# Two layers of a mixed network with a mixture of experts: the filter spectra start ahead of the routing, and eight tiles for the first expert's weights go

## The chip, the cores and the metric

The kernel runs on one core of one Trainium2 chip. The metric is the device time of one execution in microseconds (us); lower is better. The engines are named as in the profile: PE (TensorE matmul), PEld (TensorE weight load), DVE (VectorE), ACT (ScalarE), POOL (GpSimd), SP (SyncE, which only issues transfers here). Each engine works through its own queue strictly in the order in which the program was laid out.

## The reference, cut to what matters

The network has two blocks of two layers each on 256 tokens of width 1024. The first block ends in a mixture of experts: a router picks two of eight experts for each token, and each expert is a gated feed-forward network of hidden width 3584.

```python
def moe_swiglu(h, router, wg, wu, wd):
    logits = (h @ router).astype(jnp.float32)
    top_v, top_i = lax.top_k(logits, TOP_K)
    gates = jax.nn.softmax(top_v, axis=-1)
    combine = jnp.sum(jax.nn.one_hot(top_i, N_EXPERTS, dtype=jnp.float32) * gates[..., None], axis=-2)
    for e in range(N_EXPERTS):
        y = y + combine[..., e:e + 1] * swiglu(h, wg[e], wu[e], wd[e]).astype(jnp.float32)
```

The second block needs two things that depend on no token of the first: the spectra of its long filters (a small network on 256 positions, a window, a norm, a Fourier transform), and keys and values of a memory of 256 rows for its cross attention.

```python
def hyena_filter_spectra(z, window, w1, b1, w2, b2, w3, b3, freq):
    h = jnp.sin(c(freq[0]) * (z @ c(w1) + c(b1)))
    h = jnp.sin(c(freq[1]) * (h @ c(w2) + c(b2)))
    h = (h @ c(w3) + c(b3)).reshape(L, HY_ORDER, 2, HY_WIDTH) * window[:, None, None, :]
    fwd, bwd = h[:, :, 0], h[:, :, 1]
    f = jnp.concatenate([fwd, jnp.zeros((1, HY_ORDER, HY_WIDTH), F32), bwd[1:][::-1]], axis=0)
    f = f / (jnp.sum(jnp.abs(f), axis=0, keepdims=True) + EPS)
    return jnp.fft.rfft(f, axis=0)
```

## The kernel before, in words

All stages run one after the other: a front (attention, feed-forward, a recurrent layer), the mixture of experts (`st_moe`), and two layers of the second block.

**Weights.** Three pools of tiles of 512 KB serve the whole kernel: `wt` (7), `wh` (7) and `wl` (6), 20 tiles. In the dense layers a weight is loaded into `wt` and split into a high part in `wh` and a low part in `wl`. In the mixture of experts the weights are used in float32 as they come, so that `moe_fetch` loads them into the three pools in turn. One expert has 84 such tiles, and SP issues their loads in the order of use; a load waits until the tile's former user is done. For the first fetches there are eight more tiles, `early0` to `early7`, in a pool that is opened ahead of the expert loop and closed after the first call of `moe_hidden`.

**The routing** (lines 755 to 835) transposes the tokens, multiplies by the router, takes the two best, counts the tokens of each expert (`pp` L779 to L781, `pc` L800) and ranks the experts. Then `moe_select` builds a selection matrix (`sel` L949), and `moe_gather` (L962) collects the tokens of a pair of experts by eight groups of matmuls into `hT`. The experts run in the order of `ranks`; in slots 64, 64, 96, 64, 96, 64, 96, 64 tokens wide (experts 0 to 7 below). Each has four steps s: 16 tiles of gate and up weights in `moe_hidden` (8 in the last step half as wide, so three steps of 24 and one of 12 tiles with `moe_down`, 84 in all).

**The side work.** Spectra and memory keys and values are a generator, `moe_side`; `fill()` advances it by one step. Between groups of matmuls the expert loop calls `fill()` four times a step for experts of 64 slots and three times for those of 96 (none in the very first step): 12, 16, 12, 16, 12, 16, 12, 16, in all 112 calls. The spectra have 35 steps for each of the two layers, the memory 18 for each, in all 106. Inside the expert loop PE's order is pinned to the order of the program (`in_order`). What the steps of the spectra do up to the second product of the transform, with the tags of their buffers (one buffer a tag), is:

```python
w1 = s1.tile([33, 64], F32, name="hw1", tag="hw1")
w2 = s1.tile([64, 64], F32, name="hw2", tag="hw1")
zT = s1.tile([33, T], F32, name="zT", tag="hh1")
    arg = s1.tile([64, T], F32, name="arg", tag="inv")
        w3 = s1.tile([65, 512], F32, name="w3", tag="inv")
            nc.tensor.matmul(ps, h[:65, c * P:(c + 1) * P], w3[:65], start=True, stop=True)
            nc.vector.tensor_tensor(t, ps, win[:, c], op=ALU.mult)
        S = s1.tile([P, 512], F32, name="S", tag="S")
        nc.vector.tensor_tensor(S, ps, inv, op=ALU.mult)
        nc.gpsimd.tensor_tensor(S, S, skip, op=ALU.add)
        nc.gpsimd.dma_start(self.spec[i][o][:, fc], S)
```

So `w2` takes the buffer of `w1`, the two `w3` follow each other in the buffer that `arg` had, and the second `S` takes the buffer of the first, whose transfer to DRAM must have landed. All loads of the spectra are issued by POOL.

**PSUM.** `st_moe` has the banks `mm` (3), `tp` (1), `y` (2), `yc` (1) and `gs` (1). A step of the side work that asks for a bank while it rides in `fill()` gets the one that `self.ride` names, `gs` or `yc`. The routing and the gathers use `gs` as well.

Of the kernel before, what the change touches and what calls it, by code (L numbers as in the profile page):

```python
# [8 lines left out]
F32 = mybir.dt.float32  # L9
# [7 lines left out]
P = 128  # L17
# [48 lines left out]
class KB:  # L66
# [657 lines left out]
    def st_moe(self):  # L724
        nc, tc, I = self.nc, self.tc, self.I
        E, F = 8, 3584
        with tc.tile_pool(name="moc", bufs=1) as mc, tc.tile_pool(name="mot", bufs=2) as mt, self.banks(y=2, yc=1, gs=1):
            self.side = self.moe_side()
            xn = [mc.tile([P, TC, D], FR, name=f"xn{i}") for i in range(2)]
            io8 = mc.tile([P, E], F32, name="io8")  # L730
            nc.sync.dma_start(io8, I["c_iota"][:, :E])
# [103 lines left out]
            nc.vector.tensor_copy(cnti, cnt[:, E:])  # L835

            self.mo = mc, mt, xn, ios, dup
            self.homes = cycle([(self.wp, "wt"), (self.whp, "wh"), (self.wlp, "wl")])

            ranks = (0, 4, 1, 5, 2, 6, 3, 7)  # L840
# [3 lines left out]
            def weights(i):  # L844
                q = ranks[i]
                if q == 0:
                    return [I[f"moe_{n}"][0] for n in ("gate", "up", "down")]
                if ids[i] is None:
                    ids[i] = nc.values_load(idi[0:1, q - 1:q], engines=(mybir.EngineType.SP,), min_val=1, max_val=E - 1)
                return [I[f"moe_{n}"][bass.ds(ids[i], 1)].rearrange("o t p n -> (o t) p n") for n in ("gate", "up", "down")]  # L850
# [2 lines left out]
            pair = self.moe_select(ranks[:2], posr)  # L853
            for k in range(KC):
                self.moe_gather(pair, k)

            early = tc.tile_pool(name="early", bufs=1)
            ep = early.__enter__()
            self.early = iter([ep.tile([P, 1024], F32, name=f"early{i}") for i in range(8)])

            prev, scatter, nxt = None, [], None
            with self.in_order():
                for i, s in order:
                    j = i % 2
                    short = slots[i] == 64
                    jobs = {}
                    job = lambda g, f: jobs.setdefault(g, []).append(f)
                    if prev:
                        job(0, lambda o=prev: self.moe_turn(o))
                        job(1, lambda o=prev: self.moe_turn_c(o))  # L870
                    if s == 0 and prev:
                        back = self.moe_back(prev, posr, Gr, ranks[i - 1])
                        next(back)
                        job(2, lambda: next(back))
                        job(3, lambda: next(back))
                    if s == 1:
                        for g, f in enumerate(scatter):
                            job(g, f)
                    if j == 1 and i + 1 < E and s >= 2:
                        if s == 2:  # L880
                            nxt = self.moe_select(ranks[i + 1:i + 3], posr)
                        for g in range(4):
                            job(g, lambda k=4 * (s - 2) + g: self.moe_gather(nxt, k))
                    self.ride = "yc" if short and s else "gs"
                    if i or s:
                        for g in (1, 3, 4, 5) if short else (1, 3, 5):
                            job(g, self.fill)
                    one = self.moe_hidden(pair, j, weights(i), s, jobs, slots[i])
                    if not prev:
                        early.__exit__(None, None, None)  # L890
                    else:
                        scatter = self.moe_down(prev, jobs)
                    prev = one
                    if s == len(self.MOE_S) - 1 and j == 1 and i + 1 < E:
                        pair = nxt
                self.ride = "gs"
                back = self.moe_back(prev, posr, Gr, ranks[-1])
                next(back)
                self.moe_turn(prev)
                next(back)  # L900
                self.moe_turn_c(prev)
                next(back)
                self.fill(99)
                for f in self.moe_down(prev, {}):
                    f()
# [76 lines left out]

    def moe_fetch(self, src, a):

        t = next(self.early, None)
        if t is None:
            pool, tag = next(self.homes)
            t = pool.tile([P, 1024], F32, name=tag, tag=tag)
        self.nc.sync.dma_start(t, src)
        t = t.rearrange("p (a b) -> p a b", a=a)  # L990
        return [t[:, i] for i in range(a)]
# [962 lines left out]
```

## Time and profile before

| what | value |
|---|---|
| median of 3 runs | 2669.59 us (2655.94 to 2670.45) |
| the profiled execution | 2667.7 us, its span 2665.9 us, 1.8 us around it |
| PE busy | 2554.8 us, 96% of the span |
| mean granted TensorE clock | 0.979 of full speed |
| HBM read | 620.97 MB |

Matmuls are pipelined and their ends are modelled, so that a high busy share of PE does not say that PE is the bound. Where the DMA share (mean busy share of the 16 DMA engines) stands at 1.00, the stream of weights is the bound whatever PE's share is.

### The profile page before, as it was taken

To read this page: it belongs to the slowest core of one execution; us is meant where nothing else is said; L and a number is where in the kernel's file an instruction comes from. 1 tells how busy PE (TensorE), PEld (TensorE's weight loads), DVE (VectorE), ACT (ScalarE), POOL (GpSimd) and SP (SyncE) were. 2 spreads that over 40 slices of the span, in tenths; PEclk is the share of its full clock that TensorE was granted. 3 is DMA by queue.
4 is the path that set the end of the run, shared out by engine and by line. 5 is a ranking of instruction groups with operands and counts; after the bars stand their busy time and mean duration, and the time that the engine had idled before them with its cause. 6 is when DMAs were issued, how large, how long until landed. Compare 5 with 4: busy or idle time off the path is not lost. (4 is left out here: it accounts for less than half of the span.)

```text
span 2665.9 us, 34015 instructions
## 1 busy us (share of the span) xinstructions
PE 2554.8 (96%) x12437; PEld 1625.0 (61%) x12437; DVE 1146.4 (43%) x1838; ACT 1032.8 (39%) x1751; POOL 228.4 (9%) x354
## 2 busy tenths in 40 slices
PE   8999999899999999899999879999999999999999
PEld 6788877433433423354344357777777767777777
DVE  6655574222112211212122065757644657656544
ACT  6544464101101110222122065546654655546543
POOL 1000000111200211000000030100100111001000
PEclk9999997899999999899999989999999999999999
DMA  5555552799999999798988955335455544444553
GB/s 160 175 190 184 178 163 94 284 405 415 416 389 386 417 384 337 299 348 305 359 304 308 375 171 158 122 122 197 147 171 186 162 141 136 141 145 161 175 181 103
DMA packets 237218, 632.73 MB, mean 237 GB/s; under 512 B 31070, under 2 KB 38228, under 8 KB 236532
## 3 DMA queue, kind: packets, MB, share of 16 engines
q1 hardware_dynamic: 232628, 618.62, 65.0%
q0 software_dynamic: 4128, 11.67, 1.1%
q8 instruction: 100, 1.64, 0.2%
q14 instruction: 74, 0.61, 0.1%
q10 hardware_dynamic: 288, 0.19, 0.0%
HBM read 620.97 MB, written 9.44 MB: 236 GB/s over the span
## 5 line engine op out<-in xcount | busy, mean ns | idle before, releaser
L165 DVE TENSOR_TENSOR wl<-wt,wh 128x1024 fp32r<-128x1024 f32 (+2 forms) x477 | 578.6, 1219 | 323.5 <-PE mm L157 151.3
L164 ACT ACTIVATE wh<-wt 128x1024 fp32r<-128x1024 f32 (+2 forms) x477 | 495.3, 1053 | 256.2 <-PE y L158 138.0
L156 PE MATMUL mm<-wh,hTh 128*128 128x512 f32 (+2 forms) x1104 | 438.6, 398 | 4.3 <-ACT hTh L167 3.0
L158 PE MATMUL mm<-wh,hTl 128*128 128x512 f32 (+2 forms) x1104 | 434.6, 395 | 2.6 <-DVE hTl L168 2.5
L157 PE MATMUL mm<-wl,hTh 128*128 128x512 f32 (+2 forms) x1104 | 433.5, 393 | 0.4 <-DVE wl L165 0.4
L156 PEld LDWEIGHTS mm<-wh,hTh 128*128 128x128 f32 x1104 | 209.8, 190 | 54.0 <-ACT hTh L167 7.3
L158 PEld LDWEIGHTS mm<-wh,hTl 128*128 128x128 f32 x1104 | 209.3, 190 | 47.9 <-DVE hTl L168 5.2
L157 PEld LDWEIGHTS mm<-wl,hTh 128*128 128x128 f32 x1104 | 209.8, 190 | 42.9 <-issue 2.4
L1006 PE MATMUL mm<-wl,hT 128*64 128x512 f32 (+1 forms) x724 | 175.1, 556 | 3.4 <-DMA wl<-in_moe_up 2.5
L1006 PE MATMUL mm<-wt,hT 128*64 128x512 f32 (+1 forms) x692 | 162.6, 541 | 4.2 <-DMA wt<-in_moe_up 4.2
L1096 PE MATMUL y<-wh,aT 128*64 128x512 f32 x348 | 164.7, 606 | 1.4 <-DMA wh<-in_moe_down 1.3
L1006 PE MATMUL mm<-wh,hT 128*64 128x512 f32 (+1 forms) x600 | 147.4, 562 | 8.1 <-DMA wh<-in_moe_up 5.1
L156 PE MATMUL y<-wh,ah 128*128 128x512 f32 x368 | 147.3, 403 | 1.7 <-ACT ah L164 1.7
L158 PE MATMUL y<-wh,al 128*128 128x512 f32 x368 | 144.8, 400 | 0.0
L157 PE MATMUL y<-wl,ah 128*128 128x512 f32 x368 | 143.7, 396 | 0.0
L1096 PE MATMUL y<-wt,aT 128*64 128x512 f32 x292 | 138.7, 605 | 0.2 <-DMA wt<-in_moe_down 0.2
L1096 PE MATMUL y<-wl,aT 128*64 128x512 f32 x256 | 121.5, 601 | 2.4 <-DMA wl<-in_moe_down 2.3
L1006 PEld LDWEIGHTS mm<-wl,hT 128*64 128x64 f32 x724 | 48.7, 138 | 87.2 <-issue 65.1
L1014 ACT ACTIVATE sg<-mm 128x512 f32<-128x512 f32 (+1 forms) x32 | 17.4, 543 | 206.3 <-PE mm L1006 206.2
L1006 PEld LDWEIGHTS mm<-wt,hT 128*64 128x64 f32 x692 | 47.6, 138 | 76.4 <-issue 58.3
L1031 DVE COPY aT<-tp 128x512 f32<-128x512 f32 (+1 forms) x32 | 20.0, 624 | 167.9 <-PE tp L1029 167.9
L1006 PEld LDWEIGHTS mm<-wh,hT 128*64 128x64 f32 x600 | 41.7, 139 | 78.7 <-issue 61.9
(659 smaller groups left out, 3852.6 us busy)
## 6 DMA issues: line engine op xcount, KB each, us to landing
wt<-in_mlp_w SPq DMA_DIRECT2D x128, 512.0 KB, 4.4
wt<-in_w_in SPq DMA_DIRECT2D x104, 512.0 KB, 4.5
wh<-in_moe_down SPq DMA_DIRECT2D x87, 512.0 KB, 9.8
wl<-in_moe_gate SPq DMA_DIRECT2D x79, 512.0 KB, 9.5
wt<-in_moe_gate SPq DMA_DIRECT2D x78, 512.0 KB, 7.7
wl<-in_moe_up SPq DMA_DIRECT2D x78, 512.0 KB, 9.4
wt<-in_moe_down SPq DMA_DIRECT2D x73, 512.0 KB, 9.2
wt<-in_moe_up SPq DMA_DIRECT2D x71, 512.0 KB, 9.9
```

The source lines that it names most:

```text
L156: nc.tensor.matmul(ps, a[0], b[0], start=start, stop=False)
L157: nc.tensor.matmul(ps, a[0], b[1], start=False, stop=False)
L158: nc.tensor.matmul(ps, a[1], b[0], start=False, stop=stop)
L164: nc.scalar.activation(hi, src, AF.Copy)
L165: nc.vector.tensor_tensor(lo, src, hi.bitcast(F32), op=ALU.subtract)
L1006: nc.tensor.matmul(bank[i][64 * z:64 * z + 64, :W], hT[:, k, :64], gu[i][k - k0][:, z * W:(z + 1) * W], start=k == 0, stop=k == KC - 1)
L1014: nc.scalar.activation(a[:, :W], bank[0][:, :W], AF.Silu)
L1031: nc.vector.tensor_copy(o["aT"][:, :nj], pt[:, :nj * P].rearrange("p (j t) -> p j t", j=nj))
L1096: nc.tensor.matmul(y[n][64 * z:64 * z + 64], aT[:, j, 64 * z:64 * z + 64], w[j - j0][z][:, n * 512:(n + 1) * 512], start=first and j == 0, ...
```

## The change

The side work gets its first step at the head of `st_moe`, ahead of the routing in the program, and fourteen more behind the routing, ahead of the first gather. `self.ride` is `gs` for those. The pool `early` and its eight tiles are gone, so that the first fetches go to the 20 tiles of the three pools. The number of `fill()` calls in the expert loop stays.

```diff
@@ st_moe
             self.side = self.moe_side()
+            self.fill()
             xn = [mc.tile([P, TC, D], FR, name=f"xn{i}") for i in range(2)]
...
             self.mo = mc, mt, xn, ios, dup
+            self.ride = "gs"
+            self.fill(14)
             self.homes = cycle([(self.wp, "wt"), (self.whp, "wh"), (self.wlp, "wl")])
...
             pair = self.moe_select(ranks[:2], posr)
             for k in range(KC):
                 self.moe_gather(pair, k)
-
-            early = tc.tile_pool(name="early", bufs=1)
-            ep = early.__enter__()
-            self.early = iter([ep.tile([P, 1024], F32, name=f"early{i}") for i in range(8)])
...
                     one = self.moe_hidden(pair, j, weights(i), s, jobs, slots[i])
-                    if not prev:
-                        early.__exit__(None, None, None)
-                    else:
+                    if prev:
                         scatter = self.moe_down(prev, jobs)
@@ moe_fetch
-        t = next(self.early, None)
-        if t is None:
-            pool, tag = next(self.homes)
-            t = pool.tile([P, 1024], F32, name=tag, tag=tag)
+        pool, tag = next(self.homes)
+        t = pool.tile([P, 1024], F32, name=tag, tag=tag)
```

On PE the place is between the counts of the routing (`gs<-M,tri`) and the first gather (`gs<-sel,xn`). Before, the queue read:

```order
L781 MATMUL gs<-M,tri 128x8
L800 MATMUL gs<-M,tri 128x8 x2
L962 MATMUL gs<-sel,xn_3943 128x256
L962 MATMUL gs<-sel,xn_3944 128x256
...
L1006 MATMUL mm<-early_4157,hT 64x512
```

With the change it reads as follows; L1163 are the two layers of the small network, L1184 its output for two directions and two halves of the tokens, L1222 and L1232 the norm, L156 to L158 the products of the transform:

```order
L782 MATMUL gs<-M,tri 128x8
L801 MATMUL gs<-M,tri 128x8 x2
L1163 MATMUL gs<-zT,hw_3950 64x256
L1163 MATMUL gs<-hh,hw_3952 64x256
L1184 MATMUL gs<-w_4147,hh 128x512 x2
L1184 MATMUL gs<-w_4162,hh 128x512 x2
L1222 MATMUL gs<-ones,acc 128x1 x4
L1232 MATMUL gs<-ident,inv_4195 128x128 x4
L156 MATMUL gs<-pmh,dfh 128x512
...
L158 MATMUL gs<-pmh,dfl 128x512
L959 MATMUL gs<-sel,xn_3958 128x256
```

All of the matmuls of the fifteen steps (two products of six matmuls at their end) now stand in one piece ahead of the first gather, and none between two matmuls of the routing.

On POOL the place is the same stretch of the program. Before, the norm of the tokens (`ss`, `rm`, `rs`) and the scaled tokens `xn` came first:

```order
L188 TENSOR_TENSOR ss_4009<-ss 128x1
L175 TENSOR_SCALAR rm<-ss_4009 128x1
L177 TENSOR_TENSOR rs<-rm,mhalf 128x1
L786 TENSOR_SCALAR xn_3943<-x,rs 128x1024
L380 DMA win<-in_c_win 128x2x512
L382 DMA fwd<-in_c_dft 128x1024
```

With the change the first loads stand ahead of them, and all that follows to the second `S` behind them:

```order
L380 DMA win<-in_c_win 128x2x512
L382 DMA fwd<-in_c_dft 128x1024
L1152 DMA hw_3950<-in_hy_w_2 33x64
L1156 DMA zT<-in_c_zT 33x256
...
L787 TENSOR_SCALAR xn_3958<-x,rs 128x1024
L1154 DMA hw_3952<-in_hy_w_2 64x64
...
L1179 DMA w_4147<-in_hy_w_2 64x512
...
L1242 DMA spec_88<-S 128x512
L1241 TENSOR_TENSOR S<-S,skip 128x512
```

The loads of `win`, `fwd`, `hw` and `zT` moved ahead of the norm of the tokens; the order among the steps of the spectra stayed.

## Rows read from the trace of the kernel before

**Rows 1.** Windows by stage: length, busy time of each engine, clock, DMA share, GB/s.
```profile
480.00:494.00 14.00, 6.96 (x38) 6.63 (x38) 7.03 (x46) 0.37 (x2) 2.68 (x1) 0.62 0.93 378
494.00:512.20 18.20, 17.64 (x72) 8.18 (x74) 1.76 (x11) 3.79 (x8) 0.58 (x1) 0.83 0.00 1
512.20:924.60 412.40, 399.94 (x2096) 149.93 (x2092) 80.88 (x159) 50.40 (x95) 56.45 (x70) 0.99 1.01 403
817.30:924.60 107.30, 106.62 (x552) 41.50 (x548) 23.01 (x45) 15.90 (x31) 16.36 (x18) 1.00 1.01 400
924.60:1055.70 131.10, 129.26 (x772) 45.80 (x770) 22.78 (x44) 14.64 (x28) 17.59 (x20) 1.00 0.97 372
1055.70:1200.10 144.40, 132.00 (x643) 59.42 (x640) 30.17 (x57) 34.49 (x76) 8.19 (x20) 0.95 0.85 320
1200.10:1364.20 164.10, 152.88 (x858) 62.71 (x858) 31.41 (x51) 32.45 (x63) 6.49 (x16) 0.99 0.82 313
1364.20:1516.40 152.20, 139.07 (x664) 65.29 (x660) 26.76 (x38) 28.55 (x50) 7.18 (x14) 0.97 0.88 340
```

**Rows 2.** The timeline of SP's queue: start, us, line, tile.
```profile
484.26 0.33 SPq L989 DMA_DIRECT2D wh<-in_moe_up  x1
512.20 0.33 SPq L989 DMA_DIRECT2D wt<-in_moe_gate  x1
```

**Rows 3.** The timeline of PE: router, counts, first gather.
```profile
480.26 1.92 PE L769 MATMUL gs<-rt,xT 128*128 128x8 f32 x16 [0.72 <-POOL rs L177]
484.19 3.58 PE L769 MATMUL gs<-rt,xT 128*128 128x8 f32 x16 [2.01 <-DVE L L770]
490.72 0.59 PE L800 MATMUL gs<-M,tri 128*128 128x8 f32 x2 [0.26 <-DVE pos L784]
493.94 1.28 PE L962 MATMUL gs<-sel,xn 128*128 128x256 f32 x4 [2.63 <-DVE sel L949]
```

**Rows 4.** The timelines of DVE, PE and ACT: last reader of the counts, one layer of the network.
```profile
493.18 0.14 DVE L832 SCALAR_TENSOR_TENSOR cnt<-gs,cap 1x8 f32<-1x8 f32 x1
535.79 0.64 PE L1168 MATMUL yc<-zT,hw 33*64 33x256 f32 x2
539.85 0.42 ACT L339 ACTIVATE hh<-sinr 64x256 f32<-64x256 f32 x1 [4.21 <-DVE sinr L338]
```

**Rows 5.** The timelines of PE, POOL and DVE: second layer, output weights, sums, norm.
```profile
543.38 0.64 PE L1168 MATMUL yc<-hh,hw 64*64 64x256 f32 x2
546.38 0.53 POOL L1184 DMA_DIRECT2D w<-in_hy_w  x1 [1.54 <-DVE sinr L333]
562.00 1.12 PE L1189 MATMUL yc<-w,hh 65*128 65x512 f32 x2
563.17 0.69 DVE L1191 TENSOR_TENSOR f<-yc,win 128x512 f32<-128x512 f32 x1 [3.72 <-PE yc L1189]
579.98 1.26 POOL L1200 TENSOR_TENSOR acc<-acc,ab 128x512 f32<-128x512 f32 x1 [0.74 <-ACT ab L1198]
588.05 1.05 PE L1227 MATMUL yc<-ones,acc 128*128 128x1 f32 x8
598.86 1.16 PE L1237 MATMUL gs<-ident,inv 128*128 128x128 f32 x8
```

**Rows 6.** The timelines of POOL and DVE: first S, its transfer, second S.
```profile
611.53 1.38 POOL L1246 TENSOR_TENSOR S<-S,skip 128x512 f32<-128x512 f32 x1 [18.15 <-DVE S L1245]
613.22 0.57 POOL L1247 DMA_DIRECT2D spec<-S  x1 [0.30 <-POOL S L1246]
619.91 0.69 DVE L1245 TENSOR_TENSOR S<-gs,inv 128x512 f32<-128x512 f32 x1 [4.00 <-DMA spec<-S]
```

**Rows 7.** POOL's transfers, us to landing: of tile `w`; in the window 1259:1268, DMA share ahead.
```profile
DMA to landing us min/median/max: 5.1/5.5/6.8
...
DMA  0000000399400000000000948948989798999869
...
kv<-vo POOLq DMA_DIRECT2D x1, 256.0 KB, 2.7
```

## The prediction

> **What bounds the kernel now.** I read the windows by stage first. From 512.20 us, when the weights of the experts flow again, to 924.60 us the DMA share is 1.01: the stream of expert weights is the bound, and PE's 97% is matmuls that wait for tiles [rows 1]. Ahead of that the stream stands still: from 494.00 to 512.20 us the share is 0.00. SP's queue says why: the load at 484.26 us filled the last of 28 tiles (20 and the eight early ones), and the next one, at 512.20 us, waits for a tile that the first expert has used [rows 2]. Ahead of the first gather PE itself waits for the routing: of the 14 us from 480 to 494 it is busy 6.96 us, at a granted clock of 0.62 [rows 1]. From 924.60 us on the share falls to 0.97, and with the memory steps in experts 5 to 7 to 0.85, 0.82 and 0.88: there PE and the buffers bind, not the stream alone. So the time of this stage is: when the first expert's matmuls begin, plus a stretch set by DMA, plus a stretch with the memory steps. I look for what the change does to each of the three.
>
> **The first expert begins later: the sum.** The order of PE in the section on the change shows the fifteen steps' matmuls as one block between the counts and the first gather. PE goes through its queue in order, so the gather, now at 493.94 us [rows 3], waits for the whole block. Every product of the block uses the bank `gs`, of which there is one, and so each waits until the last one is read out. The block can begin when the counts have left that bank, at 493.18 + 0.14 = 493.3 us [rows 4]. Then:
>
> - *Two layers of the small network.* From the matmul to the end of the sine it took 539.85 + 0.42 - 535.79 = 4.5 us [rows 4]; twice 9.0. Six short DVE instructions of the routing now stand between those of the first layer, some 0.15 us each: 0.9. Sum 9.9, and 0.6 for the clock (below): 10.5. The second layer's weights take the buffer of the first's, but they are under way while DVE works on the first sine, and their landing (2.7 us if DMA is quiet) is hidden.
> - *Output weights, first direction.* Their buffer was `arg`'s, so POOL issues the load 546.38 - 543.38 = 3.0 us after the second layer's matmul [rows 5]; the bias row 0.5 later lands 2.7 after that, 6.2 in all, against 4.5 + 0.3 of the layer: 1.5 us remain.
> - *Two products and their readings.* 563.17 + 0.69 - 562.00 = 1.9 us each [rows 5], one behind the other for the bank; with the clock 2.7 each: 5.4.
> - *Output weights, second direction.* They wait for the second product to let go of the buffer; of the load (0.3 + 0.5 + 2.7) some 0.7 lies beside the reading of that product: 2.8.
> - *Two more products, three sums.* Product and reading 2.7; the zeroing on POOL 0.5, the absolute value on ACT 0.6, then two sums of 1.27 us with another absolute value between them, as `ab` has one buffer [rows 5]: 4.6. Together 7.3.
> - *The norm.* Matmuls of 1.05 and 1.16 us [rows 5], about 1.3 more for the clock, two short DVE instructions 0.4, a copy 0.6: 4.5. The halves for the transform are made beside it, the second half ends 1.4 later.
> - *The products and S.* The rest of the first product 1.2, its reading 0.7, POOL's sum 1.4, 0.3 to the transfer. The second `S` takes the buffer of the first and waited for its transfer (619.91, put down to the transfer issued at 613.22) [rows 6]: 2.8 with DMA quiet, and 0.7 to read the second product, which frees the bank for the gather.
>
> Sum: 10.5 + 1.5 + 5.4 + 2.8 + 7.3 + 4.5 + 1.4 + 1.2 + 0.7 + 1.4 + 0.3 + 2.8 + 0.7 = 40.5 us, so that the gather begins near 493.3 + 40.5 = 533.8 instead of 493.94: **+40 us**.
>
> Two prices are not fixed by a row. The landing of POOL's transfers: 5.1 to 6.8 us for these weights beside the stream, and 6.7 for the `S` transfer, but 2.7 in a window in which the DMA engines were idle around it [rows 6, 7]. In the block the stream stands, so I take 2.7; with 5.5, 5.5 and 6.7 the sum is 9.5 more, 50. The clock: sixteen equal matmuls took 1.92 us and 3.58 us [rows 3], and the window's mean of 0.62 lies nearest the lower level (1.2 GHz); PE is mostly idle in the block, so I count the block's matmuls near double. At the upper level the sum is 5 less, 35.
>
> All of it is laid on the end of the stage: SP has 20 tiles in flight or full, and no load goes out until the first is used. DMA has no other work, and what was idle for 18.2 us will be idle for some 55.
>
> **The eight tiles.** They cost next to nothing. Eight loads at 512 KB and 403 GB/s [rows 1] are 10.4 us, but the stream stood 18.2 us with all 28 full. With 20 the first use already frees a tile that SP may fill; the first eight tiles are used beside the gathers, one per gather group, at a pace slower than the stream fills them, so that at the ninth use the same number has come. I count 0 to 1 us; alone, without cover, it would be 10.4.
>
> **The first step ahead of the routing.** Five POOL instructions, among them loads of 1 MB, go ahead of the norm of the tokens. They wait for buffers of the layer before, which DVE and PE let go well ahead of 480 us. One split of `fwd` on ACT and DVE comes ahead of the squares and the last additions to `x`. I count 0, as POOL was idle there; a late landing would delay the routing by a few us, which the upper end holds.
>
> **What comes back later.** In the stretch set by DMA nothing: steps of the spectra under a stream at 1.01 were free [rows 1]. But the side work is fifteen calls ahead. Before, calls 71 to 106 were the memory steps: 14 in expert 5, 12 in 6, 10 in 7. With the change they are one in expert 3, 12 in 4, 16 in 5 and 7 in 6, and expert 7 has none. Priced by rows 1: expert 4 becomes like 6 (164.1 for 131.1, +33.0); expert 5 gets two more at (144.4 - 107.3) / 14 = 2.65 (+5.3); expert 3 one (+2.7); expert 6 keeps 7 of 12, 33.0 x 5/12 less (-13.7) and some 4 us of steps that are not replaced; expert 7 falls from 152.2 to between the 107.3 of expert 3 and some 115 with the next stage's first loads (-41). Sum about -18; as it is made of differences, I take 15, between bounds. Lower bound 0: the DMA idle of experts 5 to 7, 0.15 x 144.4 + 0.18 x 164.1 + 0.12 x 152.2 = 69.5 us, belongs to the memory's weight blocks, which hold tiles of all three pools, and goes with them unchanged. Upper bound 30, if expert 6 too loses what its five empty calls cost.
>
> **Sum.** 2667.7 (the profiled execution, 2 us under the median of 2669.59) + 40 + 0 - 15 = **2693 us**. Bounds: 35 - 30 = +5 and 50 - 0 = +50.
>
> The Trainium skill speaks against this change in Perfetto Trace Analysis, Matmuls: independent groups of matmuls should rotate through PSUM banks, so that reading one overlaps the next. Here the trace shows the rule's other side, readings of 0.69 us that follow their products [rows 5]. With a second bank, by that rule, the gather need not wait for the second `S`, and the sum would be about 5 us less.
>
> **Rivals.**
> - *The block costs more and gives nothing back.* POOL's transfers land as they did beside the stream, and the memory's idle time moves unchanged: 2667.7 + 50 = 2718. For it: all landings of these tiles that the trace has. Against it: the quiet one at 2.7 us [rows 7].
> - *The block lies in the routing's gaps.* If the small network ran while PE waits for the routing, with its 7.0 us of idle time there (14.0 - 7.0 [rows 1]), the two layers' 10.5 us would be hidden, the delay 30, and with 15 to 25 back the time 2673 to 2683: no change. Against it: the order, in which the block is behind the counts, and the bank `gs`. The Trainium skill has this hope in Perfetto Trace Analysis, Optimization Strategy: regimes with different bounds may gain by interleaving.
> - *Faster.* The memory steps, fifteen calls earlier, lie under a stream that is still the bound, and the 69.5 us of idle DMA vanish: 2667.7 + 40 - 69.5 = 2638. It decides once more than 54 us come back. Against it: expert 6, where the steps lie beside a 96-slot expert, has the lowest share, 0.82, and expert 4 is one as well [rows 1].
>
> **How the numbers follow.** Forecast 0.62 (own range 2680 to 2710), costlier 0.18, gaps 0.12, faster 0.08. A measurement of this kernel can tell about 0.5% (13 us) from no change. Slower by over that: 0.59 of the forecast, all of the costlier case, 0.01 of the gaps: 0.78. Within: 0.03 and 0.11: 0.14. Faster: 0.08. The range 2674 to 2717 leaves out the faster case and the tail of the costlier one.
>
> **What would show it.** After: first gather near 534 instead of 494 us; ahead of it PE busy for a small part of some 40 us, and a DMA share of 0.00 for about 55 us; the second `S` waits for `spec<-S`, landed in about 2.8 us; the last expert's window near 110 us at a DMA share of 1.00. Wrong: a first gather before 520, or experts 4 to 7 together more than 45 us shorter than before (592).

## The result, and the profile after

The changed kernel takes 2705.1 us (median of 4 runs, 2703.74 to 2707.17) against 2668.67 us (4 runs, 2655.94 to 2670.45): ratio 1.0152, 95% interval 1.0127 to 1.0177, **slower**, though by less than 2%: 36.4 us between the medians, 34 to 47 us by the interval. The profiled execution took 2705.91 us, 38.2 more than that of before. The forecast was 2693, slower, range 2674 to 2717: sign and range held, the size was 12 us short.

PE around the routing in the timeline of the changed kernel: counts (L801), the fifteen steps (L1163 to L156), the first gather (L959) and the first expert's first matmul (L1001). In the brackets stands the idle time before a matmul and what ended it:

```profile
487.09 0.59 PE L801 MATMUL gs<-M,tri 128*128 128x8 f32 x2 [0.26 <-DVE pos L785]
489.76 1.11 PE L1163 MATMUL gs<-zT,hw 33*64 33x256 f32 x2 [2.08 <-DVE cnt L833]
495.01 1.11 PE L1163 MATMUL gs<-hh,hw 64*64 64x256 f32 x2 [4.14 <-ACT hh L339]
501.54 2.04 PE L1184 MATMUL gs<-w,hh 65*128 65x512 f32 x2 [5.41 <-DMA w<-in_hy_b]
504.37 2.08 PE L1184 MATMUL gs<-w,hh 65*128 65x512 f32 x2 [0.78 <-DVE f L1186]
509.92 2.05 PE L1184 MATMUL gs<-w,hh 65*128 65x512 f32 x2 [3.48 <-DMA w<-in_hy_b]
512.75 2.08 PE L1184 MATMUL gs<-w,hh 65*128 65x512 f32 x2 [0.78 <-DVE f L1186]
517.67 1.87 PE L1222 MATMUL gs<-ones,acc 128*128 128x1 f32 x8 [2.84 <-POOL acc L1195]
...
522.82 0.79 PE L156 MATMUL gs<-pmh,dfh 128*128 128x512 f32 x1 [0.68 <-ACT inv L1233]
...
531.76 1.22 PE L959 MATMUL gs<-sel,xn 128*128 128x256 f32 x4 [2.24 <-DVE S L1240]
...
534.70 1.97 PE L1001 MATMUL mm<-wt,hT 128*64 128x512 f32 x2
```

The gather comes 531.76 - 487.09 = 44.7 us behind the counts, where it came 493.94 - 490.72 = 3.2 us behind them [rows 3]. The first idle stretch in between (2.08 us) ends with the routing's last reader of the bank (`cnt`), every later one with something of the spectra. On SP's queue the last load of the first twenty and the next one:

```profile
473.84 0.39 SPq L984 DMA_DIRECT2D wh<-in_moe_up  x1
539.07 0.34 SPq L984 DMA_DIRECT2D wt<-in_moe_gate  x1
```

For 65 us no load of weights was issued, where it was 28 us [rows 2]. The windows of the changed kernel (columns as in [rows 1]): the block, the first expert, then experts 4 to 7 from the end of one to the end of the next (start of its last `sg` on ACT):

```profile
487.10:531.80 44.70, 20.83 (x43) 10.31 (x43) 15.96 (x57) 5.93 (x11) 14.17 (x18) 0.50 0.06 19
531.80:617.20 85.40, 83.58 (x384) 33.05 (x386) 11.36 (x21) 10.53 (x19) 8.10 (x11) 0.96 0.90 349
...
967.10:1138.90 171.80, 155.70 (x852) 61.69 (x848) 30.87 (x60) 32.12 (x72) 8.19 (x20) 0.96 0.77 289
1138.90:1290.20 151.30, 140.07 (x683) 66.53 (x680) 36.33 (x57) 41.90 (x80) 8.55 (x20) 0.97 0.91 351
1290.20:1454.90 164.70, 157.77 (x872) 65.17 (x868) 21.81 (x33) 22.99 (x41) 5.12 (x10) 1.00 0.84 320
1454.90:1553.40 98.50, 93.97 (x478) 32.12 (x476) 10.91 (x20) 5.44 (x10) 0.00 (x0) 1.00 1.03 419
```

In the block PE is busy 20.8 of 44.7 us at a granted clock of 0.50 and the DMA share is 0.06, the spectra's own small transfers. Experts 4 to 7 took 171.8, 151.3, 164.7 and 98.5 us, together 586.3 against 591.8 [rows 1]. PE is busy for 547.5 of these, before for 553.2: its idle time is the same, 38.8 and 38.6. The 38.2 us add up, to rounding: the gather comes 41.5 us later behind the counts, the first expert takes 2.9 longer from its first matmul, experts 1 to 7 together take 3.7 less, the stages behind them 1.2 more, and the counts come 3.6 earlier (the last is no part of the change, see the end).

### The profile page after: what moved, and what is told of

It reads as the page before. It is cut to its first block, busy times and chain, and to the rows that moved or that the text cites. A ratio compares the mean times of both kernels' runs of the same rounds, so it can differ in the third digit from the quotient of the medians.

```text
span 2704.1 us, 34030 instructions
## 1 busy us (share of the span) xinstructions
PE 2570.4 (95%) x12437; PEld 1628.7 (60%) x12437; DVE 1145.7 (42%) x1838; ACT 1033.3 (38%) x1752; POOL 229.0 (8%) x354
## 5 line engine op out<-in xcount | busy, mean ns | idle before, releaser
L165 DVE TENSOR_TENSOR wl<-wt,wh 128x1024 fp32r<-128x1024 f32 (+2 forms) x477 | 578.3, 1218 | 321.1 <-PE mm L157 151.3
L156 PE MATMUL mm<-wh,hTh 128*128 128x512 f32 (+2 forms) x1104 | 438.6, 398 | 3.5 <-ACT hTh L167 2.1
L158 PE MATMUL mm<-wh,hTl 128*128 128x512 f32 (+2 forms) x1104 | 435.2, 395 | 2.6 <-DVE hTl L168 2.5
L156 PEld LDWEIGHTS mm<-wh,hTh 128*128 128x128 f32 x1104 | 210.1, 190 | 52.4 <-ACT hTh L167 5.5
L158 PEld LDWEIGHTS mm<-wh,hTl 128*128 128x128 f32 x1104 | 209.6, 190 | 48.0 <-DVE hTl L168 5.4
L1001 PE MATMUL mm<-wh,hT 128*64 128x512 f32 (+1 forms) x736 | 180.3, 551 | 2.0 <-DMA wh<-in_moe_up 1.8
L1001 PE MATMUL mm<-wl,hT 128*64 128x512 f32 (+1 forms) x700 | 168.8, 546 | 5.9 <-DMA wl<-in_moe_up 5.9
L1091 PE MATMUL y<-wt,aT 128*64 128x512 f32 x348 | 165.7, 607 | 4.9 <-DMA wt<-in_moe_down 4.8
L1001 PE MATMUL mm<-wt,hT 128*64 128x512 f32 (+1 forms) x612 | 156.0, 566 | 2.4 <-DMA wt<-in_moe_up 2.4
L156 PE MATMUL y<-wh,ah 128*128 128x512 f32 x368 | 147.2, 402 | 1.7 <-ACT ah L164 1.7
L1091 PE MATMUL y<-wl,aT 128*64 128x512 f32 x292 | 139.8, 602 | 7.0 <-DMA wl<-in_moe_down 6.8
L158 PE MATMUL y<-wh,al 128*128 128x512 f32 x368 | 144.9, 400 | 0.0
L1091 PE MATMUL y<-wh,aT 128*64 128x512 f32 x256 | 123.8, 609 | 0.8 <-DMA wh<-in_moe_down 0.8
L1001 PEld LDWEIGHTS mm<-wh,hT 128*64 128x64 f32 x736 | 50.5, 138 | 87.0 <-issue 71.0
L1001 PEld LDWEIGHTS mm<-wl,hT 128*64 128x64 f32 x700 | 48.3, 138 | 80.8 <-issue 54.7
L1001 PEld LDWEIGHTS mm<-wt,hT 128*64 128x64 f32 x612 | 42.7, 139 | 73.0 <-issue 55.1
```

The costliest lines, as they stand in the source:

```text
L156: nc.tensor.matmul(ps, a[0], b[0], start=start, stop=False)
L158: nc.tensor.matmul(ps, a[1], b[0], start=False, stop=stop)
L165: nc.vector.tensor_tensor(lo, src, hi.bitcast(F32), op=ALU.subtract)
L1001: nc.tensor.matmul(bank[i][64 * z:64 * z + 64, :W], hT[:, k, :64], gu[i][k - k0][:, z * W:(z + 1) * W], start=k == 0, stop=k == KC - 1)
L1091: nc.tensor.matmul(y[n][64 * z:64 * z + 64], aT[:, j, 64 * z:64 * z + 64], w[j - j0][z][:, n * 512:(n + 1) * 512], start=first and j == 0, ...
```

## The experiments

The theory: PE's order puts the fifteen steps' serial chain between counts and gather, through the one bank `gs`; the eight tiles and the early loads cost nothing; later little comes back. The rivals: the eight tiles carry a part of the loss; the fifteen steps ahead give back 15 us, as I forecast, and the block costs more than 40; the loss is the waiting itself, whatever bank it uses.

All kernels are read by the same marks: from the counts (start of L801, or L800) to the first gather, to the first expert matmul, to the end of the first expert, and the length of experts 1 to 7, in us from each profile. The ratio is to the kernel before, run beside each (medians 2664.48, 2667.84 and 2658.69 us for the three groups).

| kernel | median us | ratio, 95% interval | gather | matmul | first expert's end | experts 1 to 7 |
|---|---|---|---|---|---|---|
| before | 2668.67 | | 3.2 | 6.2 | 85.8 | 939.9 |
| changed | 2705.1 | 1.0152, 1.0127 to 1.0177 | 44.7 | 47.6 | 130.1 | 936.2 |
| 1 early gone | 2662.99 | 0.9999, 0.998 to 1.0019 | 3.2 | 6.2 | 87.3 | 948.0 |
| 2 first step | 2661.64 | 0.9993, 0.9974 to 1.0012 | 3.2 | 6.2 | 88.0 | 942.4 |
| 3 bank yc | 2667.64 | 1.001, 0.9993 to 1.0027 | 4.9 | 8.0 | 97.9 | 931.9 |
| 4 ahead, no block | 2680.86 | 1.008, 1.0048 to 1.0112 | 3.2 | 6.2 | 108.5 | 939.3 |
| 5 block, 16 calls less | 2724.1 | 1.021, 1.0181 to 1.0239 | 44.5 | 47.5 | 126.0 | 965.0 |
| 6 three banks | 2680.27 | 1.0052, 1.0028 to 1.0076 | 5.2 | 33.4 | 111.3 | 933.7 |
| 7 four calls | 2674.4 | 1.0031, 1.0006 to 1.0055 | 9.7 | 12.6 | 94.1 | 943.9 |
| 8 in the first step | 2677.67 | 1.0045, 1.0025 to 1.0065 | 3.2 | 6.2 | 116.1 | 931.1 |
| 9 same place | 2702.75 | 1.0168, 1.0138 to 1.0199 | 44.8 | 47.7 | 126.0 | 946.6 |
| 10 yc, same place | 2672.29 | 1.0045, 1.0024 to 1.0066 | 4.9 | 8.0 | 94.5 | 943.1 |
| 11 w3 early | 2691.62 | 1.0141, 1.0106 to 1.0175 | 40.5 | 43.5 | 126.0 | 935.5 |

**1. The eight tiles.** The kernel before without them:

```diff
-            early = tc.tile_pool(name="early", bufs=1)
-            ep = early.__enter__()
-            self.early = iter([ep.tile([P, 1024], F32, name=f"early{i}") for i in range(8)])
```

> The kernel before without the eight early tiles, nothing else. Theory of the block (the whole loss is the block of fifteen steps in front of the first gather): about 2669 us, at most 2 us over the kernel before, the SP load that waits for the first used tile still near 512 us and the stream idle some 10 us longer ahead of it, but nothing later in the first expert. Theory of the tiles (they are a part of the loss): +10 us, 2679, all of it in the first expert.

Measured 0.9999: no loss; the upper end of the interval is 5 us, so 10 is excluded. The expectation had the next load wrong (near 512 us, the stream idle some 10 us longer). SP's queue of this kernel:

```profile
465.37 0.38 SPq L981 DMA_DIRECT2D wh<-in_moe_up  x1
489.01 0.34 SPq L981 DMA_DIRECT2D wt<-in_moe_gate  x1
```

The next load goes out 10.4 us behind the counts (478.62), in the kernel before 21.5 us behind them [rows 2, 3]: a used early tile was filled by nobody, a used tile of the three pools is refilled at once. The stream starts 11.1 us sooner behind the counts, and eight loads are worth 10.4: the two cancel. The prediction itself had this reason (with 20 tiles the first use already frees one), the expectation did not use it.

**2. The first step.** The changed kernel without the two lines `self.ride = "gs"` and `self.fill(14)`.

> The changed kernel without the fourteen calls behind the counts: only the first step (its loads) stays ahead of the routing, and the eight tiles are gone. Theory of the block: 2669 us, 0 to 2 over the kernel before, first gather near 494 us. Theory of the tiles: 2679. If the megabyte of loads on the queue of POOL ahead of the routing costs something, the first gather is late by that much with the matmuls ahead of it in the same order.

Measured 0.9993, the gather 3.2 us behind the counts. No cost of the loads ahead of the routing shows (the interval is -7 to +3 us). So the loss is in the fourteen calls.

**3. Another bank.**

```diff
-            self.ride = "gs"
+            self.ride = "yc"
             self.fill(14)
```

> The changed kernel, but the fourteen calls take the bank yc, which nobody uses before the third expert, in place of gs. The order of TensorE then has the gathers between the products of the block. Theory of the one bank: the first gather within 8 us of the counts instead of 44.7, the first expert begins 30 to 40 us earlier than in the changed kernel, and the time is 2670 to 2685 us. Rival (the work of the block itself costs, whatever bank it has): the products wait in TensorE's queue all the same and the time stays above 2695.

Measured 1.001 (-2 to +7 us): the loss is gone, with all of the same work ahead of the first expert's end. PE in this kernel's timeline:

```profile
479.76 0.59 PE L801 MATMUL gs<-M,tri 128*128 128x8 f32 x2 [0.27 <-DVE pos L785]
480.28 1.11 PE L1163 MATMUL yc<-hh,hw 64*64 64x256 f32 x2
484.63 1.39 PE L959 MATMUL gs<-sel,xn 128*128 128x256 f32 x4 [3.24 <-DVE sel L946]
486.59 1.22 PE L959 MATMUL gs<-sel,xn 128*128 128x256 f32 x4 [0.56 <-ACT hT L962]
487.74 1.97 PE L1001 MATMUL mm<-wt,hT 128*64 128x512 f32 x2
...
492.16 1.13 PE L1184 MATMUL yc<-w,hh 65*128 65x512 f32 x2
492.73 1.03 PE L959 MATMUL gs<-sel,xn 128*128 128x256 f32 x4
...
500.85 1.10 PE L1184 MATMUL yc<-w,hh 65*128 65x512 f32 x2 [0.19 <-DMA w<-in_hy_b]
```

The first layer runs ahead of the counts (at 466.6 us), the second right behind them, and the output products stand between gathers and expert matmuls: the wait for the weights' landing that was 5.41 us in the changed kernel is none here, the next 0.19 instead of 3.48. The bank did not only make PE wait, it fixed the order in which the program was laid out: a user of `gs` that is written first must let go of it before the next.

**6. Three banks, but those of the expert.** The same line with `"mm"`.

> The changed kernel, with the fourteen calls on the three banks mm in place of gs. The gathers then stand between the products of the block, but the first expert's sums need two of these banks and come behind the block's products. If what costs is that the first gather waits, this is as good as with the bank yc: 2665 to 2672. If what costs is that the first expert's matmuls, the first users of the tiles, come behind the block, most of the loss stays: 2690 to 2702, the first expert matmul some 30 us later than with yc.

Both readings missed: +14 us (7 to 20). The gathers are early (5.2 us), the first expert matmul comes 33.4 us behind the counts, 25 later than with `yc`, and 11 us more were paid than there (0.42% of 2667, with an uncertainty of 8). So it is the delay of the expert's first matmul that is paid, not that of the gather. Once all gathers are done and twenty tiles are full, this kernel goes through the first expert in 111.3 - 33.4 = 77.9 us; with `yc` it takes 97.9 - 8.0 = 89.9, as the block's products lie in it. So of 25.4 us of delay 13.4 are left at the end of the first expert: between these two kernels, a block ahead costs its length less what it costs inside.

**7. Four calls.** `self.fill(4)` in place of 14.

> The changed kernel with four calls behind the counts instead of fourteen (the two layers of the small network). Theory of the block: the first gather waits for the part of the block that is left, from 489.8 to about 500 us in the changed kernel's trace, so 6 to 11 us over the kernel before: 2671 to 2676. Rival (a fixed price of the new place of the side work, whatever its length): over 2690.

Measured +8 us (2 to 15). In the profile:

```profile
495.33 1.11 PE L1163 MATMUL gs<-hh,hw 64*64 64x256 f32 x2 [4.14 <-ACT hh L339]
497.07 1.22 PE L959 MATMUL gs<-sel,xn 128*128 128x256 f32 x4 [0.63 <-DVE arg L1166]
```

The gather goes as soon as `gs` is read, 6.4 us later than before. The loss grows with what stands ahead of the gather.

**8. The same block behind the gathers.** The fourteen calls as jobs of the four gaps of the first expert's first step (4, 4, 3, 3), bank `gs`.

> The changed kernel with the same fourteen calls not ahead of the first gather but in the four gaps of the first expert's first step (4, 4, 3 and 3), still with the bank gs. The first gather then comes 3 us behind the counts. If the loss is that no tile is used while the block lasts, part of it goes: the stream runs again some 20 us sooner and 12 to 25 us remain, 2677 to 2690. If the wait itself on TensorE is the loss wherever it stands, it stays near 2702.

Measured +12 us (7 to 17). The first expert ends 116.1 us behind the counts instead of 130.1. Tiles are used between the waits: SP's first refill goes out 10.5 us behind the counts, in the changed kernel 52.0, and two later stands of 10.1 and 9.8 us follow.

**11. Two waits of the block.**

```diff
-                w3 = s1.tile([65, 512], F32, name="w3", tag="inv")
+                w3 = s1.tile([65, 512], F32, name="w3", tag="inv" if d else "f11")
```

> The changed kernel, but the output weights of the first direction go into a buffer that is free from the start (f11), so that their load need not wait for the buffer arg, and those of the second direction into arg's, so that they need not wait for the first direction's products. My sum had 1.5 and 2.8 us for these two waits; the changed kernel's trace has waits of 5.41 and 3.48 us in their places. By the trace the gather comes 6 to 9 us sooner behind the counts (36 to 39 us instead of 44.7) and the time is 2696 to 2700; by my sum 4 us sooner, 2701; if the waits only move to another thing that is late, nothing changes.

The ratio, 1.0141, cannot tell 4 us from none. The profile can (PE, and one line of ACT):

```profile
486.17 1.11 PE L1163 MATMUL gs<-hh,hw 64*64 64x256 f32 x2 [4.15 <-ACT hh L339]
490.69 0.42 ACT L339 ACTIVATE hh<-sinr 64x256 f32<-64x256 f32 x1 [4.58 <-DVE sinr L338]
491.21 2.04 PE L1184 MATMUL gs<-w,hh 65*128 65x512 f32 x2 [3.93 <-issue]
494.04 2.08 PE L1184 MATMUL gs<-w,hh 65*128 65x512 f32 x2 [0.78 <-DVE f L1186]
496.90 2.08 PE L1184 MATMUL gs<-w,hh 65*128 65x512 f32 x2 [0.78 <-DVE f L1186]
```

The gather comes 40.5 us behind the counts, 4.2 sooner: my sum's 1.5 + 2.8, not the trace's 5.4 + 3.5. Of the wait of 5.41 us that was put down to the load, 3.93 stays: the sine of the second layer (`hh`) ends only at 490.69 + 0.42 = 491.11 us.

**Being ahead: 4, 5, 9, 10.** Kernel 4 is the kernel before with two steps a call in the first expert and in the second's first step. Kernel 5 is the changed kernel without sixteen calls, kernel 9 without fifteen; 10 is 3 without the same fifteen:

```diff
-                    if i or s:
-                        for g in (1, 3, 4, 5) if short else (1, 3, 5):
+                    if (i, s) > (0, 3):
+                        for g in (5,) if (i, s) == (1, 0) else (1, 3, 4, 5) if short else (1, 3, 5):
```

> The kernel before, with two steps of the side work a call instead of one in the first expert and in the first step of the second: sixteen steps ahead, as with the change, but with no block ahead of the gather. My forecast's term: the memory steps in experts 4 to 6 instead of 5 to 7 give back 15 us, 2654. Rival (each memory step costs the same wherever it stands, as TensorE is busy there): 2669, within 4 us, experts 4 to 7 together 585 to 595 us long, with the last one near 100.

> The changed kernel without the sixteen calls of the first expert and of the first step of the second: the block of fourteen stands ahead of the gather as before, but later the side work is no longer ahead, and the memory steps lie in experts 5 to 7 as in the kernel before. If being ahead gives back the 15 us of my forecast, this takes 15 us more than the changed kernel, 2717. If it gives back nothing (the gain in the last expert is paid in the fifth), it is as long as the changed kernel within 5 us, 2697 to 2707, with experts 5 to 7 near 144, 164 and 152 us.

> The changed kernel without fifteen of the calls that follow the block (the twelve of the first expert and three of the four in the second expert's first step), so that from there on every step of the side work stands in the same place as in the kernel before; the run without sixteen calls stood one step off and met new collisions on the bank gs. The block alone then remains, at 41 to 43 us ahead of the first expert. If being ahead gives back 15 us as I forecast, this is 15 us over the changed kernel, 2720. If it gives back about 4, as the experts' lengths of the changed kernel say, 2705 to 2712.

> The same fifteen calls left out, with the block on the bank yc: every step from the second expert on in the place that it has in the kernel before, and the fifteen first steps between gathers and matmuls of the first expert. Theory of the block: no more than 5 us from the kernel before, 2663 to 2673, first expert's end 86 to 92 us behind the counts (before 85.8). If being ahead gives something back, this is longer than the run with yc alone by as much: 4 or 15 us.

Kernel 4 lost 13 to 30 us, which neither reading had. Its first expert takes 22.7 us longer (PE busy 14.0 more and idle 8.7 more), its second 9.6 (3.4 and 6.2): the doubled calls bring the steps' own matmuls and also waits for their chains. Its experts 2 to 7 took 815.9 us against 826.1 before, 10.2 less. Kernel 5 seemed to say that being ahead is worth 15 and more, but it stood one call off, and that made waits of its own. In its expert 3, where PE waits 6.76 us for ACT's reading of the gather (`hT`):

```profile
959.04 0.72 PE L959 MATMUL gs<-sel,xn 128*128 128x256 f32 x4
...
967.35 0.63 ACT L164 ACTIVATE pmh<-pmf 128x512 fp32r<-128x512 f32 x1 [9.80 <-POOL pmf L1202]
968.40 1.22 PE L959 MATMUL gs<-sel,xn 128*128 128x256 f32 x4 [6.76 <-ACT hT L962]
```

ACT should read the gather out of `gs`, but ahead of it in ACT's queue stands a split of the spectra (`pmh`) that waits for POOL. Kernel 9, in step again, is the clean partner of the changed kernel and 10 that of 3. The experts 1 to 7 of the kernels that are ahead and in step (changed, 3, 6, 8, 11) took 931.1 to 936.2 us, of those that are not (before, 1, 2, 9, 10) 939.9 to 948.0: means 933.7 and 944.0, some 10 us. (Kernel 2 is one step ahead; without it the second mean is 944.4. Kernel 4 with its doubled calls, 5 and 7 with their steps in other places are left out.) The first expert pays 3.4 (97.9 - 94.5) to 4.2 (130.12 - 125.95) of it back for its twelve steps. Net 6 to 7; the ratios say 4 (1.0168 - 1.0152) and 9 us (1.0045 - 1.001), each with an uncertainty of 7 to 10. The means mix profiles; the before that I summed against happens to be the shortest of its group.

Kernel 10 also shows what the fifteen steps cost with a bank of their own, which I had put at no more than 5: its first expert ends 94.5 us behind the counts, those of kernels 1 and 2 at 87.6 in the mean, 7 us; in all it lost 6 to 18 us.

No kernel beats the one before by more than its interval.

## Why the prediction was right, and where it was short

- **Order and place of the block: right.** The gather at 531.8 us (forecast 534), 41.5 us later behind the counts (forecast 40). Kernels 2, 3 and 7 show that the fourteen calls in `gs`, and nothing else of the change, make the loss.
- **The sum, part by part.** Two layers with the first load: 501.54 - 489.76 = 11.8 (forecast 10.5 + 1.5). Two products and the second load: 8.4 (5.4 + 2.8). Two products and the sums: 7.8 (7.3). Norm: 5.2 (4.5). From the first product to the gather: 8.9 (8.5). Together 42.0 for 40.5. The price of a quiet landing, 2.7 us [rows 7], held: `spec<-S` issued at 528.23, the second `S` at 531.02. The lower clock, which I took from [rows 1, 3], was granted all through (0.50, that is 1.2 of 2.4 GHz, with PE busy for less than half of the block).
- **The eight tiles and the first step: right**, 0 each (kernels 1 and 2). My reason for the tiles held as well: the stream stood with all of them full, and without them the first use already let it start again, 11.1 us sooner.
- **What comes back: the step that failed.** I took 15 us; against the profile before it was 3.7 over experts 1 to 7, and that is 11.3 of the 13.2 us by which the profiled execution exceeds the sum (38.2 - 25). Against the kernels in step it was some 10, and the first expert took 3 to 4 back. The range held because its upper end allowed for nothing coming back. The terms: expert 4 +40.6 (forecast +33.0), 5 +6.9 (+5.3), 3 +3.1 (+2.7), 7 -53.6 (-41), and **6 +0.6, where I had "expert 6 keeps 7 of 12, 33.0 x 5/12 less (-13.7)" and 4 more**. My prices did not keep the work: fifteen steps arrived for 41.0 us (33.0 + 5.3 + 2.7) and the same fifteen left for 54.7 (13.7 + 41). The steps are not even either: of a layer's 18 steps eight hold a product of 24 matmuls, the first of them in the sixth step. Expert 6 of the kernel before, in the groups by line (times: sum, mean in ns):

```profile
L156 PE MATMUL gs<-wh,memTh 128*128 128x512 f32 x32 | 13.0, 407 | 1.1 <-DVE x L254 1.1
L158 PE MATMUL gs<-wh,memTl 128*128 128x512 f32 x32 | 12.7, 395 | 0.0
L157 PE MATMUL gs<-wl,memTh 128*128 128x512 f32 x32 | 12.6, 395 | 0.0
...
L156 PE MATMUL yc<-wh,memTh 128*128 128x512 f32 x8 | 3.3, 408 | 0.0
```

and of the changed kernel:

```profile
L156 PE MATMUL gs<-wh,memTh 128*128 128x512 f32 x32 | 13.0, 407 | 1.1 <-DVE x L254 1.1
...
L156 PE MATMUL yc<-wh,memTh 128*128 128x512 f32 x16 | 6.5, 408 | 0.0
```

Eight of L156 are one product, and a product is (13.0 + 12.7 + 12.6) / 4 = 9.6 us of PE. Expert 6 had five and now has six; experts 4 to 7 had 0, 4, 5, 7 and now have 4, 6, 6, 0. Part of that is my mark: the last two or three calls of an expert stand behind its last gate and up matmuls, and so fall into the next expert's window. Counted by calls the products are 0, 5, 5, 6 before and 4, 8, 4, 0 with the change, so that expert 6 lost steps by calls and gained a product by its window. All sixteen still lie in experts 4 to 7. There PE's idle time stayed (38.6 and 38.8 us), and the time fell by no more than PE's work, 5.5 us for 5.7. The prediction had named that case as its lower bound, but argued it from DMA. The products alone do not price each expert: expert 5 has two more, some 19 us of PE, and took 6.9 longer. How the rest divides no run shows.
- **The second bank.** I had worked out 5 us for it, and kernel 3 got back nearly all of the loss. The Trainium skill's rule (Perfetto Trace Analysis, Matmuls), that independent groups of matmuls rotate through PSUM banks, agrees with that run as far as gathers and block then have two banks (1.001 for 1.0152). I had counted only the last wait for a reading, not that the bank decides which products may stand between which.
- **Rivals.** "Gaps" did not come true in the change. With `yc` it does in part: the two layers run beside the routing and the gather comes 1.7 us later, not 30; the loss goes, but no gain follows. The Trainium skill's hope (Perfetto Trace Analysis, Optimization Strategy), that interleaving regimes may gain, is borne out by that run only so far. "Costlier" is as far from the measured 2705 us (2718) as the forecast, and half of its reason held: little came back, but the landings stayed quiet. "Faster" fell: experts 4 to 7 are 5.5 us shorter, not 69.5.

## What to carry to other kernels

When work is moved into a gap, look which PSUM bank it takes and who needs that bank next: a serial chain in the bank of the critical step became that step's delay here, whatever the engine's idle time, and one free bank undid it. Price moved steps by the instructions in them, not by their number, check that what leaves one place is priced like what arrives at the other, and ask whether the bound of the place that they leave is the bound of the place that they go to. An early buffer that nobody refills also delays the next refill: here eight tiles, worth 10.4 us of stream, delayed it by 11.1 us and gained nothing.

## What the runs showed of the hardware that I had not expected

The profiles reach the counts between 478.2 and 493.4 us, though the kernels are the same up to the first loads of the side work. In the recurrent layer, the last stage ahead of the routing, the granted clock falls to the lower level (0.50, 1.2 GHz) in some profiles and stays at the upper one (1.00, 2.4 GHz) in others, with PE busy for the whole stretch, and for the 20 us ahead of it, in both. Why it falls stays open. The kernel before, and kernel 1 in the same stretch (columns as in [rows 1]), both in that layer:

```profile
410.00:420.00 10.00, 10.00 (x30) 7.12 (x29) 1.11 (x2) 3.80 (x14) 0.00 (x0) 0.50 0.00 0
```

```profile
410.00:420.00 10.00, 10.00 (x58) 7.94 (x57) 2.23 (x4) 5.30 (x18) 0.00 (x0) 1.00 0.00 0
```

Differences under some 10 us between two single profiles were therefore read from the counts on, not from the start.
